# Two expert layers with a dense gate map: another layout of the map in PSUM, another plan of the choose stage, and later gathered sums

## The chip, the cores and the metric

The kernel runs on one core of a Trainium2 chip. A core has five engines with a queue each: TensorE (PE; its weight loads are shown apart as PEld), VectorE (DVE), ScalarE (ACT), GpSimd (POOL) and SyncE (SP, which here only issues DMAs). They share the on-chip memory SBUF; matrix products land in PSUM, eight banks of 2 KiB per partition, from where VectorE and ScalarE read them. The metric is the device time of one execution in microseconds; a time is the median of several runs.

## The reference

Two blocks work on 512 tokens of width 1024, in float32: the first with gated linear attention and a sliding window, the second with two other attentions. Each ends in a PEER layer, and the change lies there. A layer has 8 heads, and each head picks 16 of 128 x 128 = 16384 experts, so that every token has 128 experts with a gate each:

```python
def peer_layer(xn, w_pq, sub_keys, expert_u, expert_v):
    ...
    scores = jnp.einsum('thpd,hpkd->thpk', qp, sub_keys).astype(jnp.float32)
    s_top, i_top = lax.top_k(scores, PEER_TOPK)
    cand = (s_top[:, :, 0, :, None] + s_top[:, :, 1, None, :]).reshape(t, PEER_HEADS, PEER_TOPK * PEER_TOPK)
    cand_idx = (i_top[:, :, 0, :, None] * PEER_NKEYS + i_top[:, :, 1, None, :]).reshape(...)
    best, pos = lax.top_k(cand, PEER_TOPK)
    idx = jnp.take_along_axis(cand_idx, pos, axis=-1)
    gate = jax.nn.softmax(best, axis=-1).astype(xn.dtype)
    ...
        u = expert_u[ib]
        h = jax.nn.gelu(jnp.einsum('lkd,ld->lk', u, xb), approximate=False)
        return jnp.einsum('lk,lkd->ld', gb * h, expert_v[ib])
```

## The kernel before

**Two ways through the experts.** For the first 384 tokens (TD) a layer goes through all 16384 experts densely: 128 chunks of 128 experts. For each chunk it multiplies the chunk of u with the tokens, applies gelu, multiplies with a map of gates that is zero where a token has not picked an expert, and multiplies the result with the chunk of v. The last 128 tokens are done by gathering: four sets of 32 tokens, whose 128 experts per token are fetched by indirect DMAs, 32 fetches of u rows and 32 of v rows per set (NSET = 4, tile `gr`).

**Split operands.** Dense products are made of float32 operands in two parts, a high part rounded to the format fp32r, and a low part, the rest. `mm3` (lines 285 to 287) issues three matmuls: high by high, low by high, high by low. One chunk of u is a *unit* of 8 x 3 = 24 matmuls of 128x384. Its weights are split when they have come in: ScalarE writes the high part (`whi`, line 222), and VectorE or GpSimd the low part (`wlo`, line 231). `unit` keeps one split unit ahead.

**choose**, once per layer, has three sorts of work that run beside each other:
- `best` finds the top 16 of the scores on VectorE, and `select` (one call per 128 tokens, `pick` around it) the 16 of 256 candidates, with their two keys i1 and i2 and the gates, all on VectorE. Its `turn` transposes keys and gates on TensorE (float32, three transposes), and ScalarE and VectorE write them as i1T, i2T and the high and low parts of the gate, ghi and glo.
- `maps` builds the gate map in halves of 16 tokens, 24 halves per layer. `one_hots` makes four tables per half on VectorE (lines 1258, 1259, 1261, 1262): `o1`, `ah`, `al`, `o2`, the last of which is shown as `o` at line 1262. `gate_map` then issues 32 matmuls of 128x128 in fp16 (lines 1275 and 1276) into four banks `pg`, four tokens in each, and after each bank ScalarE copies it into `stage` (line 1278). Two halves make a `stage`, which goes to DRAM.
- `uahead` does 56 of the 128 u chunks ahead of the main loop, 52 of them in choose, so that TensorE has work while VectorE selects. The low part is made by VectorE except where the call says GpSimd.

**What sets the order.** Every engine runs its queue in order, and choose writes the queues by a plan: `tv` and `tp` are the expected times of VectorE and TensorE. After each piece of `select` or `one_hots` the generator yields its cost, `tv` grows by it, and `fill(tv - behind)` issues units (4.2 each) until TensorE's time has come up; `flush` then issues the TensorE work that VectorE has prepared (`turn`, and `dense` at 1.9). `force` issues waiting work at once where a buffer must come free.

**main_loop** has 131 steps, one for each v unit (two chunks' halves) and for the late u chunks, 72 of 128. A step in order: `weigh` (line 1637, the low part `wl` of the weighted activations of the step before, on VectorE, after ScalarE's high part `wh` of line 1690), `low_u` (line 1589, the low part of the next late unit, on VectorE), `high_v`, issues of gathers, one gathered step, `low_v` (line 1610), the unit's matmuls, more gathered steps, the weighting by the map (line 1687), then the products with v, and `flush_later`. A gathered step is a reduction over the fetched u row (line 1319) or an accumulation of the fetched v row (line 1331, tile `acc`) on VectorE. After the last accumulation of a set `fin` sums the partitions by quads on TensorE (line 1338, 8 small matmuls) and VectorE adds the result to xT (`upd_t`: line 443 in the first layer, 470 in the second). `fin` is handed to `soon`, and runs at the next `flush_later`: at the end of the step, or at once when the next set's first step (`ustep` with j = 0) comes up.

Of the kernel before, what the change touches and what calls it, by code (L numbers as in the profile page):

```python
# [8 lines left out]
F32 = mybir.dt.float32  # L9
# [168 lines left out]
class Kern:  # L178
    def __init__(self, ctx, tc, ins, cat, outs, upto, dbg):
        self.ctx, self.tc, self.nc = ctx, tc, tc.nc  # L180
        self.ins, self.cat, self.outs, self.upto, self.dbg = ins, cat, outs, upto, dbg
        self.alt, self.alt2 = 0, 0

        self.ahead = [c for c in range(P) if c // 4 % 2 == 0 and c < 112]
        self.late = [c for c in range(P) if c not in self.ahead]
        self.ua_last = 4
        self.ua_end, self.behind = 6, 0.5
# [962 lines left out]
    def select(self, i, sv, si, sp, sp2, out, later, force):  # L1150
# [47 lines left out]
        V.tensor_tensor(t1[:, 0:8], ge, dl[:, :, :, None].to_broadcast(B4), op=ALU.mult)  # L1198
        V.tensor_tensor(t1[:, 8:16], ge, self.offD[:, None, :, :].to_broadcast(B4), op=ALU.mult)
        yield 3.4  # L1200
        for w in (8, 4, 2):
            V.tensor_add(t1[:, :, 0:w, :], t1[:, :, 0:w, :], t1[:, :, w:2 * w, :])
        yield 2.4
        i1 = sp.tile([P, 8, 16], F32, tag="i1", name="i1")
        i2 = sp.tile([P, 8, 16], F32, tag="i2", name="i2")
# [5 lines left out]
                        op=ALU.is_equal)  # L1211
        yield 2.3
        V.tensor_tensor(ge, ge, ix[:, :, 1, :, None].to_broadcast(B4), op=ALU.mult)
# [3 lines left out]
        yield 4.0  # L1217
# [3 lines left out]
        V.tensor_tensor(gate, gate, sm[:, :, None].to_broadcast([P, 8, 16]), op=ALU.mult)  # L1221
        yield 0.8
# [12 lines left out]
        def turn():  # L1235
            pt = self.pb()
            for n, src in enumerate((i1, i2, gate)):
                self.transpose(pt[:, n * P:(n + 1) * P], src.rearrange("p a b -> p (a b)"))
            s = slice(i * P, (i + 1) * P)
            i1T, i2T, ghi, glo = out  # L1240
# [8 lines left out]
    def one_hots(self, t0, sel, sp, sp2, made):  # L1249


        V = self.nc.vector
        B4 = [P, 8, P, 2]
        io = self.iotaM[:, None, :, :].to_broadcast(B4)
        i1T, i2T, ghi, glo = [t[:, t0:t0 + 16].rearrange("p (q f) -> p q f", f=2)[:, :, None, :] for t in sel]
# [4 lines left out]
        yield 2.4  # L1260
        V.tensor_tensor(al, o1, glo.to_broadcast(B4), op=ALU.mult)  # L1261
        V.tensor_tensor(o2, io, i2T.to_broadcast(B4), op=ALU.is_equal)  # L1262
        yield 2.3
        made += [ah, al, o2]

    def gate_map(self, oh, stage, half):

        S, PE = self.nc.scalar, self.nc.tensor
        ah, al, o2 = oh
        for q in range(4):  # L1270
            pg = self.pb()
            for f in range(4):
                o = pg.rearrange("p (i f) -> p i f", f=4)[:, :, f]
                n, m = 2 * q + f // 2, f % 2
                PE.matmul(o, ah[:, n, :, m], o2[:, n, :, m], start=True, stop=False)  # L1275
                PE.matmul(o, al[:, n, :, m], o2[:, n, :, m], start=False, stop=True)
            tt = half * 16 + q * 4
            S.activation(stage[:, :, tt:tt + 4], pg.rearrange("p (i f) -> p i f", f=4), AF.Copy, scale=2.0 ** -15)

    def gather_steps(self, h, un, vn, gw, gb, upd_t):  # L1280
# [5 lines left out]
        for n in range(NSET):  # L1286
# [37 lines left out]
            def vstep(j, n=n, t0=t0, st=st):  # L1324
# [9 lines left out]
                if j == 31:  # L1334
# [7 lines left out]
                    self.soon(fin)  # L1342
# [31 lines left out]
    def choose(self, h, hd, nq, scores, keys_src, pu, hscr, gscr, steps, prep, gelp, mk2):  # L1374
# [6 lines left out]
        self.bank, self.soon, self.flush_later = self.pb, lambda f: f(), lambda: None  # L1381
# [4 lines left out]
        sel = [cst.tile([P, T], F16, name=n) for n in ("i1T", "i2T", "ghi", "glo")]  # L1386
# [9 lines left out]
        def uahead(eng=V):  # L1396
            nonlocal ahead, tp, tv
            ph = self.pa()
# [79 lines left out]
        del qall, keys  # L1478
        for t, n in ((self.offM, "off"), (self.offD, "offd"), (self.iotaJ, "iota16")):
            V.tensor_copy(t, self.c(n)[:, :, None].to_broadcast([P, 16, 16]))  # L1480
# [52 lines left out]
    def main_loop(self, h, pu, pv, upd, steps, start_next, finish, gscr, hscr, uahead, pools):  # L1533

# [90 lines left out]
        def flush_later():  # L1625
            while later:
                later.pop(0)()

        self.bank, self.soon, self.flush_later = lambda: turn(ubank), later.append, flush_later
# [27 lines left out]
        for s in range(NC + 3):  # L1657
# [4 lines left out]
            weigh()  # L1662
# [5 lines left out]
            gathered(min(qs, nd + 1))  # L1668
            low_v(s - 2)
# [28 lines left out]
            flush_later()  # L1698
# [553 lines left out]
```

## Time and profile before

| what | value |
|---|---|
| median of 3 runs | 3509.58 us (3507.26 to 3523.71) |
| profiled execution, its own time | 3514.7 us |
| span of that execution | 3512.9 us |
| TensorE busy | 3373.0 us, 96% |
| its weight loads (beside it) | 2950.5 us, 84% |
| VectorE busy | 2602.4 us, 74% |
| ScalarE busy | 1357.5 us, 39% |
| GpSimd busy | 926.6 us, 26% |
| choose of the first layer, from its last top-k on | 676 to 1009 us |
| choose of the second layer, likewise | 2280 to 2609 us |

The profile is one execution, taken by the hardware profiler. A row of the waits names the engine and line that waited, what it waited for, and the time in total, the number of waits and the longest. A row of a stretch gives the busy time of TensorE, the weight loads, VectorE, ScalarE and GpSimd with the number of instructions in brackets, then the clock granted to TensorE as a share of the full one, the share of the DMA engines' time, and GB/s. A row in time begins with the start and the duration in us; matmuls are pipelined, so that the distance of two starts tells their rate and the duration does not. `pb<-o,ah` reads: writes tile pb, reads o and ah; L is a line of the kernel.

### The profile page before, as it was taken

The page shows a single profiled execution, that of the slowest core. Times are in us where ns is not written, and L with a number is a line of the kernel's source. Part 1 is how long each engine was busy: PE and PEld are TensorE (multiplying, and loading weights), DVE is VectorE, ACT ScalarE, POOL GpSimd, SP SyncE. Part 2 cuts the span into 40 slices and gives each one's busy share as a digit, 9 for nine tenths or more (in the row PEclk, how much of TensorE's full clock was granted, in tenths as well). Part 3 has the DMA queues.
Part 4 walks back from the last instruction along what each step waited for, and adds up shares of the span by engine and source line. Part 5 has one row for each costly group of instructions (what it writes and reads, how often), then busy time and mean ns, then how long its engine had stood idle before and what let it go on. Part 6 is the DMA issues. An engine that isn't in the chain of part 4 may idle for free. (4 is left out here: it accounts for less than half of the span.)

```text
span 3512.9 us, 48336 instructions
## 1 busy us (share of the span) xinstructions
PE 3373.0 (96%) x17772; PEld 2950.5 (84%) x17772; DVE 2602.4 (74%) x5342; ACT 1357.5 (39%) x2497; POOL 926.6 (26%) x792
## 2 busy tenths in 40 slices
PE   9999999899989999999999999989989999999998
PEld 7768888799978888888888768879978888888887
DVE  4466665778878887888864685788878878788873
ACT  4445223234443333333334444324443333333332
POOL 1422004200013433443422401400004434344431
PEclk9999999999999999999999999999999999999999
DMA  4211673255689999899972201235689999899971
GB/s 135 78 37 47 237 249 102 78 184 183 213 290 345 328 347 332 318 351 330 355 259 77 78 19 39 79 130 186 210 259 351 354 334 335 327 343 335 350 296 66
DMA packets 321790, 787.49 MB, mean 224 GB/s; under 512 B 27392, under 2 KB 156800, under 8 KB 321424
## 3 DMA queue, kind: packets, MB, share of 16 engines
q1 hardware_dynamic: 247568, 515.36, 40.8%
q0 software_dynamic: 73984, 269.05, 22.1%
q8 instruction: 139, 2.28, 0.3%
q14 instruction: 99, 0.81, 0.1%
HBM read 709.59 MB, written 74.45 MB: 223 GB/s over the span
## 5 line engine op out<-in xcount | busy, mean ns | idle before, releaser
L1311 POOL DMA_INDIRECT gr<-in_pn_dram,gset x256 | 316.6, 1237 | 1149.4 <-DVE hd L1319 926.5
L287 PE MATMUL pa<-hh,wlo 128*128 128x384 f32 (+2 forms) x1536 | 545.9, 355 | 43.3 <-DVE wlo L231 42.3
L285 PE MATMUL pa<-hh,whi 128*128 128x384 f32 (+2 forms) x1536 | 550.6, 358 | 5.8 <-ACT whi L222 4.0
L286 PE MATMUL pa<-hl,whi 128*128 128x384 f32 (+2 forms) x1536 | 543.9, 354 | 5.9 <-POOL hl L544 4.8
L1311 POOL DMA_INDIRECT gr<-in_pm_dram,gset x256 | 328.2, 1282 | 439.7 <-DVE acc L1331 293.2
L285 PE MATMUL pa<-vh,wh 128*128 128x512 f32 x1024 | 401.9, 392 | 0.0
L286 PE MATMUL pa<-vl,wh 128*128 128x512 f32 x1024 | 400.9, 392 | 0.4 <-DVE vl L1610 0.4
L287 PE MATMUL pa<-vh,wl 128*128 128x512 f32 x1024 | 400.7, 391 | 0.0
L287 PE MATMUL pb<-hh,wlo 128*128 128x384 f32 x1152 | 389.3, 338 | 5.2 <-DVE wlo L1589 3.9
L231 DVE TENSOR_TENSOR wlo<-wraw,whi 128x1024 fp32r<-128x1024 f32 x189 | 234.7, 1243 | 213.9 <-ACT whi L222 213.3
L285 PE MATMUL pb<-hh,whi 128*128 128x384 f32 x1152 | 392.0, 340 | 0.5 <-ACT whi L1583 0.5
L286 PE MATMUL pb<-hl,whi 128*128 128x384 f32 x1152 | 388.5, 337 | 0.0
L287 PEld LDWEIGHTS pa<-hh,wlo 128*128 128x128 f32 x1536 | 293.8, 191 | 72.5 <-DVE wlo L231 49.5
L1610 DVE TENSOR_TENSOR vl<-vraw,vh 128x512 fp32r<-128x512 f32 x512 | 333.3, 692 | 5.0 <-ACT vh L1602 5.0
L1331 DVE SCALAR_TENSOR_TENSOR acc<-gr,hd,acc 128x1024 f32<-128x1024 f32 x248 | 317.8, 1281 | 24.9 <-DMA gr<-in_pm_dram,gset 23.3
L1319 DVE CUSTOM_DVE_ANT_0 gr<-gr,ht 128x1024 f32<-128x1024 f32 x256 | 309.3, 1220 | 19.8 <-DMA gr<-in_pn_dram,gset 19.8
L285 PEld LDWEIGHTS pa<-hh,whi 128*128 128x128 f32 x1536 | 294.4, 192 | 30.5 <-ACT whi L222 5.5
L286 PEld LDWEIGHTS pa<-hl,whi 128*128 128x128 f32 x1536 | 293.7, 191 | 29.3 <-POOL hl L544 6.3
L1602 ACT CAST vh<-vraw 128x512 fp32r<-128x512 f32 x512 | 291.7, 618 | 0.8 <-PE pb L287 0.7
L222 ACT CAST whi<-wraw 128x1024 fp32r<-128x1024 f32 x243 | 253.7, 1044 | 79.3 <-PE pa L286 39.1
L1690 ACT CAST wh<-gel 128x384 fp32r<-128x384 f32 x144 | 73.9, 513 | 426.6 <-DVE gel L1687 426.0
L287 PEld LDWEIGHTS pa<-vh,wl 128*128 128x128 f32 x1024 | 193.1, 189 | 40.6
(443 smaller groups left out, 6723.9 us busy)
## 6 DMA issues: line engine op xcount, KB each, us to landing
vraw<-in_pv_dram SPq DMA_DIRECT2D x256, 512.0 KB
uraw<-in_pu_dram SPq DMA_DIRECT2D x138, 512.0 KB
wraw<-in_pu_dram SPq DMA_DIRECT2D x118, 512.0 KB
wraw<-in_wT_dram SPq DMA_DIRECT2D x97, 512.0 KB
gscrp<-stage SPq DMA_DIRECT2D x24, 2048.0 KB
gt<-gscrp SPq DMA_DIRECT2D x64, 768.0 KB
ada<-in_wadaT_dram SPq DMA_DIRECT2D x48, 512.0 KB
hscrp<-gel SPq DMA_DIRECT2D x112, 192.0 KB
```

Of the source, the lines that this page charges most:

```text
L222: self.nc.scalar.copy(hi, raw)
L231: lo_eng.tensor_sub(lo, raw, hi.bitcast(F32))
L285: nc.tensor.matmul(out, l[0], r[0], start=start, stop=False, **kw)
L286: nc.tensor.matmul(out, l[0], r[1], start=False, stop=False, **kw)
L287: nc.tensor.matmul(out, l[1], r[0], start=False, stop=stop, **kw)
L1311: G.indirect_dma_start(out=u, out_offset=None, in_=tab, in_offset=bass.IndirectOffsetOnAxis(ap=self.gset[n][:, 1, j:j + 1].bitcast(I32), a ...
L1319: V.tensor_tensor_reduce(u, u, st["ht"], 1.0, 0.0, ALU.mult, ALU.add, st["hd"][:, j:j + 1])
L1331: V.scalar_tensor_tensor(st["acc"], v, w, st["acc"], op0=ALU.mult, op1=ALU.add)
L1602: S.copy(hi, vraw[u][:, c * 512:(c + 1) * 512])
L1610: V.tensor_sub(lo, raw[:, c * 512:(c + 1) * 512], vs[u][c].bitcast(F32))
L1690: S.copy(wh, gel)
```

## The change

1. In `gate_map` each token's 128 columns go to PSUM next to each other; before, the four tokens of a bank were interleaved word by word. ScalarE's copy reads the bank with the other stride, so that `stage` is the same.
2. `select` writes keys and the two parts of the gate in fp16 itself, and `turn` turns the four by fp16 matmuls against an identity, with one ScalarE copy into one tile `sel`. Before: three float32 transposes, three ScalarE copies, one VectorE operation.
3. The plan: `select` and `one_hots` yield more often, the cost is taken at 1.0 in place of 1.05, `behind` is 1.5 in place of 0.5.
4. `uahead` gives the low part to GpSimd when `tv` is over `tp` by more than 2.8.
5. `fin` is issued three steps later, at the end of a step.
6. `weigh` stands behind the step's first gathered step, in place of ahead of `low_u`.

```diff
@@ select
         V.tensor_tensor(t1[:, 0:8], ge, dl[:, :, :, None].to_broadcast(B4), op=ALU.mult)
+        yield 2.25
         V.tensor_tensor(t1[:, 8:16], ge, self.offD[:, None, :, :].to_broadcast(B4), op=ALU.mult)
-        yield 3.4
+        yield 1.2
...
-        i1 = sp.tile([P, 8, 16], F32, tag="i1", name="i1")
-        i2 = sp.tile([P, 8, 16], F32, tag="i2", name="i2")
+        i1, i2, gh, gl = [sp.tile([P, 8, 16], F16, tag=n, name=n) for n in ("i1", "i2", "gh", "gl")]
...
+        if i * P < TD:
+            V.tensor_scalar(gh, gate, 32768.0, None, op0=ALU.mult)
+            V.scalar_tensor_tensor(gl, gate, 32768.0, gh, op0=ALU.mult, op1=ALU.subtract)
...
         def turn():
             pt = self.pb()
-            for n, src in enumerate((i1, i2, gate)):
-                self.transpose(pt[:, n * P:(n + 1) * P], src.rearrange("p a b -> p (a b)"))
...
-            S.copy(i1T[:, s], pt[:, 0:P])
-            S.copy(i2T[:, s], pt[:, P:2 * P])
-            S.activation(ghi[:, s], pt[:, 2 * P:3 * P], AF.Copy, scale=32768.0)
-            V.scalar_tensor_tensor(glo[:, s], pt[:, 2 * P:3 * P], 32768.0, ghi[:, s], op0=ALU.mult, op1=ALU.subtract)
+            for n, src in enumerate((i1, i2, gh, gl)):
+                PE.matmul(pt[:, n * P:(n + 1) * P], src.rearrange("p a b -> p (a b)"), self.ident16, start=True, stop=True)
+            S.copy(out[:, :, i * P:(i + 1) * P], pt.rearrange("p (a b) -> p a b", b=P))
@@ one_hots
         V.tensor_tensor(o1, io, i1T.to_broadcast(B4), op=ALU.is_equal)
+        yield 1.25
         V.tensor_tensor(ah, o1, ghi.to_broadcast(B4), op=ALU.mult)
-        yield 2.4
+        yield 1.15
         V.tensor_tensor(al, o1, glo.to_broadcast(B4), op=ALU.mult)
+        yield 1.15
         V.tensor_tensor(o2, io, i2T.to_broadcast(B4), op=ALU.is_equal)
-        yield 2.3
+        yield 1.15
@@ gate_map
             for f in range(4):
-                o = pg.rearrange("p (i f) -> p i f", f=4)[:, :, f]
+                o = pg[:, f * P:(f + 1) * P]
...
-            S.activation(stage[:, :, tt:tt + 4], pg.rearrange("p (i f) -> p i f", f=4), AF.Copy, scale=2.0 ** -15)
+            S.activation(stage[:, :, tt:tt + 4], pg.rearrange("p (f i) -> p i f", f=4), AF.Copy, scale=2.0 ** -15)
@@ gather_steps
-                    self.soon(fin)
+                    self.soon(fin, 3)
@@ choose
-        def uahead(eng=V):
+        def uahead(eng=None):
             nonlocal ahead, tp, tv
+            eng = eng or (G if tv > tp + 2.8 else V)
...
             for cost in f(i):
-                tv += cost * 1.05
+                tv += cost
@@ main_loop
-        def flush_later():
-            while later:
-                later.pop(0)()
+        def soon(f, n=0):
+            later.append([n, f])
+
+        def flush_later(step=0):
+            for e in list(later):
+                if e[0] <= 0:
+                    later.remove(e)
+                    e[1]()
+                e[0] -= step
...
-            weigh()
             low_u(s + 1)
...
             gathered(min(qs, nd + 1))
+            weigh()
...
-            flush_later()
+            flush_later(1)
```

How the queues change is shown at three places. A row is a line of the kernel, an operation, what it writes and reads, and its shape. First VectorE in the first layer's choose, at the thirteenth and fourteenth half of the gate map (the tables o, ah, al of `one_hots` and low parts wlo), before:

```order
L231 TENSOR_TENSOR wlo<-wraw,whi 128x1024
L1261 TENSOR_TENSOR al<-o_8213,glo 128x2048
L1262 TENSOR_TENSOR o_8216<-iotaM,i2T 128x2048
L1258 TENSOR_TENSOR o_8296<-iotaM,i1T 128x2048
L1259 TENSOR_TENSOR ah<-o_8296,ghi 128x2048
L1261 TENSOR_TENSOR al<-o_8296,glo 128x2048
L1262 TENSOR_TENSOR o_8299<-iotaM,i2T 128x2048
L1258 TENSOR_TENSOR o_8345<-iotaM,i1T 128x2048
L1259 TENSOR_TENSOR ah<-o_8345,ghi 128x2048
L1261 TENSOR_TENSOR al<-o_8345,glo 128x2048
L1262 TENSOR_TENSOR o_8348<-iotaM,i2T 128x2048
```

and after:

```order
L1257 TENSOR_TENSOR o_8065<-iotaM,sel 128x2048
L1259 TENSOR_TENSOR ah<-o_8065,sel 128x2048
L1261 TENSOR_TENSOR al<-o_8065,sel 128x2048
L1263 TENSOR_TENSOR o_8068<-iotaM,sel 128x2048
L231 TENSOR_TENSOR wlo<-wraw,whi 128x1024
L1257 TENSOR_TENSOR o_8148<-iotaM,sel 128x2048
L1259 TENSOR_TENSOR ah<-o_8148,sel 128x2048
L1261 TENSOR_TENSOR al<-o_8148,sel 128x2048
L1263 TENSOR_TENSOR o_8151<-iotaM,sel 128x2048
L231 TENSOR_TENSOR wlo<-wraw,whi 128x1024
```

Before, the low parts end here, and the second half follows the first with no unit between; after, a low part stands behind each half, so that TensorE has a unit between two halves. Over the whole choose TensorE's last run of halves with no unit between has 14 halves before and 6 after in the first layer, 16 and 9 in the second.

Second GpSimd, from the last operation ahead of the first layer's choose to the first set of gathers (wlo are low parts, gr the fetched rows), before:

```order
L1298 TENSOR_TENSOR hr<-hh,hl 128x128
L231 TENSOR_TENSOR wlo<-wraw,whi 128x1024 x10
L1311 DMA gr<-in_pn_dram,gset_4703 128x1024 x32
L1311 DMA gr<-in_pm_dram,gset_4703 128x1024 x32
L1311 DMA gr<-in_pn_dram,gset_4704 128x1024 x32
L1311 DMA gr<-in_pm_dram,gset_4704 128x1024 x32
```

and after:

```order
L1299 TENSOR_TENSOR hr<-hh,hl 128x128
L231 TENSOR_TENSOR wlo<-wraw,whi 128x1024 x18
L1312 DMA gr<-in_pn_dram,gset_4703 128x1024 x5
L231 TENSOR_TENSOR wlo<-wraw,whi 128x1024 x3
L1312 DMA gr<-in_pn_dram,gset_4703 128x1024 x27
L1312 DMA gr<-in_pm_dram,gset_4703 128x1024 x32
```

Eleven more low parts stand here, eight ahead of the first fetch and three behind the fifth. In the second layer there are as many; on VectorE as many fewer, 171 in place of 193 over the kernel.

Third VectorE in the main loop, where the second set of gathered tokens in the first layer ends (line 443 adds the quad sums to xT), before:

```order
L1687 TENSOR_TENSOR gel<-gel,gt 128x384
L1637 TENSOR_TENSOR wl<-gel,wh 128x384
L1589 TENSOR_TENSOR wlo<-uraw,whi 128x1024
L1331 SCALAR_TENSOR_TENSOR acc<-gr,hd,acc 128x1024
L1610 TENSOR_TENSOR vl<-vraw,vh 128x512 x2
L1331 SCALAR_TENSOR_TENSOR acc<-gr,hd,acc 128x1024
L443 TENSOR_TENSOR xT<-pb,xT 128x8x32
L1319 ISA gr,hd<-gr,ht 128x1024
L1319 ISA hd 128x1
L1687 TENSOR_TENSOR gel<-gel,gt 128x384
L1637 TENSOR_TENSOR wl<-gel,wh 128x384
```

and after, from the same step on:

```order
L1699 TENSOR_TENSOR gel<-gel,gt 128x384
L1594 TENSOR_TENSOR wlo<-uraw,whi 128x1024
L1332 SCALAR_TENSOR_TENSOR acc<-gr,hd,acc 128x1024
L1649 TENSOR_TENSOR wl<-gel,wh 128x384
L1615 TENSOR_TENSOR vl<-vraw,vh 128x512 x2
L1332 SCALAR_TENSOR_TENSOR acc<-gr,hd,acc 128x1024
...
L1615 TENSOR_TENSOR vl<-vraw,vh 128x512 x2
L1699 TENSOR_TENSOR hb<-hb,gt 128x384
L443 TENSOR_TENSOR xT<-pb,xT 128x8x32
L1320 ISA gr,hd<-gr,ht 128x1024
```

The addition of line 443 has moved from right behind the last accumulation to 22 rows later. At the head of the step wl (line 1637, after: 1649) stood ahead of the low part wlo (1589, after: 1594), and now stands behind it and behind one accumulation.

## Rows read from the trace of the kernel before

**Rows 1.** waits of TensorE, whole span: total us, times, longest us
```profile
PE pa L287 <- DVE wlo L231: 42.3, 17, 15.6
PE pb L1275 <- DVE o L1262: 28.3, 26, 1.5
PE pb L1338 <- DVE acc L1331: 17.8, 5, 6.1
PE pb L287 <- DVE wlo L1589: 3.9, 2, 2.0
```

**Rows 2.** stretches of choose: us, then busy us by engine, clock, DMA share, GB/s
```profile
676.00:1009.00 333.00, 302.03 (x1987) 293.98 (x1986) 276.21 (x660) 140.52 (x219) 7.51 (x6) 0.97 0.59 187
2280.00:2609.00 329.00, 292.32 (x1925) 282.97 (x1924) 282.87 (x728) 137.04 (x215) 12.65 (x7) 0.98 0.58 184
680.00:720.00 40.00, 26.16 (x140) 25.84 (x139) 26.92 (x146) 7.14 (x10) 0.00 (x0) 0.83 0.28 93
2290.00:2330.00 40.00, 24.40 (x131) 23.95 (x130) 28.48 (x163) 6.32 (x10) 0.00 (x0) 0.83 0.28 92
760.00:780.00 20.00, 16.50 (x79) 15.87 (x79) 16.53 (x45) 7.49 (x11) 6.96 (x5) 0.83 0.80 266
```

**Rows 3.** waits of TensorE in 676:1009, then in 2280:2609; columns as in 1
```profile
PE pa L287 <- DVE wlo L231: 18.1, 5, 13.8
PE pb L1275 <- DVE o L1262: 11.8, 11, 1.1
...
PE pa L287 <- DVE wlo L231: 19.1, 5, 15.6
PE pb L1275 <- DVE o L1262: 16.5, 15, 1.5
```

**Rows 4.** TensorE in time at 858.6 us, and line 1275's loads (ns min/median/max)
```profile
858.57 0.34 PE L286 MATMUL pa<-hl,whi 128*128 128x384 f32 x1
...
858.92 0.28 PE L1275 MATMUL pb<-o,ah 128*128 128x128 f16 x1
859.00 0.31 PE L1276 MATMUL pb<-o,al 128*128 128x128 f16 x1
859.11 0.31 PE L1275 MATMUL pb<-o,ah 128*128 128x128 f16 x1
...
L1275 PEld LDWEIGHTS <-ah x768: 96/135/135, 835.9 to 2610.1; 128*128 128x128 f16 x192
```

**Rows 5.** line 1278 on ScalarE: ns min/median/max
```profile
L1278 ACT ACTIVATE stage<-pb x192: 597/598/602, 837.0 to 2610.6; 128x512 f32<-128x512 f32 x192
```

**Rows 6.** VectorE in time in the first layer's tail of choose
```profile
967.73 1.22 DVE L1258 TENSOR_TENSOR o<-iotaM,i1T 128x2048 f16<-128x2048 f16 x1
...
972.47 1.22 DVE L1258 TENSOR_TENSOR o<-iotaM,i1T 128x2048 f16<-128x2048 f16 x1
```

**Rows 7.** line 231 by engine: ns min/median/max, first and last start
```profile
L231 DVE TENSOR_TENSOR wlo<-wraw,whi x189: 1205/1226/1660, 12.2 to 2639.4; 128x1024 fp32r<-128x1024 f32 x189
L231 POOL TENSOR_TENSOR wlo<-wraw,whi x48: 2349/2406/2852, 60.8 to 2285.3; 128x1024 fp32r<-128x1024 f32 x48
```

**Rows 8.** VectorE, then GpSimd, in time near 1880 us; line 1610 on the page
```profile
1881.79 4.68 DVE L1610 TENSOR_TENSOR vl<-vraw,vh 128x512 fp32r<-128x512 f32 x2 [1.64 <-ACT vh L1602]
...
1880.72 5.21 POOL L231 TENSOR_TENSOR wlo<-wraw,whi 128x1024 fp32r<-128x1024 f32 x2 [79.20 <-PE pb L287]
...
L1610 DVE TENSOR_TENSOR vl<-vraw,vh 128x512 fp32r<-128x512 f32 x512 | 333.3, 692 | 5.0 <-ACT vh L1602 5.0
```

**Rows 9.** stretches of the main loops; columns as in 2
```profile
1200.00:1250.00 50.00, 47.58 (x230) 41.55 (x230) 40.10 (x61) 18.32 (x35) 19.34 (x16) 0.97 0.92 339
1400.00:1450.00 50.00, 43.86 (x208) 38.60 (x207) 37.26 (x56) 17.03 (x32) 18.30 (x15) 0.93 0.81 296
...
3400.00:3450.00 50.00, 48.42 (x245) 44.05 (x244) 24.63 (x35) 16.07 (x29) 0.00 (x0) 0.97 0.39 136
```

**Rows 10.** waits of VectorE, whole span: total us, times, longest us
```profile
DVE wl L1637 <- ACT wh L1690: 199.1, 252, 3.5
```

More of the change, by code (lines that the diff above doesn't have):

```diff
@@ L186, in __init__ @@
         self.ua_last = 4
-        self.ua_end, self.behind = 6, 0.5
+        self.ua_end, self.behind = 6, 1.5
     def dump(self, name, t):
@@ L1198, in select @@
         V.tensor_tensor(t1[:, 0:8], ge, dl[:, :, :, None].to_broadcast(B4), op=ALU.mult)
+        yield 2.25
         V.tensor_tensor(t1[:, 8:16], ge, self.offD[:, None, :, :].to_broadcast(B4), op=ALU.mult)
-        yield 3.4
+        yield 1.2
         for w in (8, 4, 2):
             V.tensor_add(t1[:, :, 0:w, :], t1[:, :, 0:w, :], t1[:, :, w:2 * w, :])
-        yield 2.4
-        i1 = sp.tile([P, 8, 16], F32, tag="i1", name="i1")
-        i2 = sp.tile([P, 8, 16], F32, tag="i2", name="i2")
+            yield 0.8
+        i1, i2, gh, gl = [sp.tile([P, 8, 16], F16, tag=n, name=n) for n in ("i1", "i2", "gh", "gl")]
         jr = sp.tile([P, 8, 16], F16, tag="jr", name="jr")
@@ L1211, in select @@
                         op=ALU.is_equal)
+        yield 2.0
+        V.tensor_tensor(ge, ge, ix[:, :, 1, :, None].to_broadcast(B4), op=ALU.mult)
         yield 2.3
-        V.tensor_tensor(ge, ge, ix[:, :, 1, :, None].to_broadcast(B4), op=ALU.mult)
         for w in (8, 4, 2):
@@ L1216, in select @@
         V.tensor_add(i2, ge[:, :, 0, :], ge[:, :, 1, :])
-        yield 4.0
+        yield 1.9
         force(exp)
@@ L1236, in turn @@
             pt = self.pb()
-            for n, src in enumerate((i1, i2, gate)):
-                self.transpose(pt[:, n * P:(n + 1) * P], src.rearrange("p a b -> p (a b)"))
-            s = slice(i * P, (i + 1) * P)
-            i1T, i2T, ghi, glo = out
-            S.copy(i1T[:, s], pt[:, 0:P])
-            S.copy(i2T[:, s], pt[:, P:2 * P])
-            S.activation(ghi[:, s], pt[:, 2 * P:3 * P], AF.Copy, scale=32768.0)
-            V.scalar_tensor_tensor(glo[:, s], pt[:, 2 * P:3 * P], 32768.0, ghi[:, s], op0=ALU.mult, op1=ALU.subtract)
+            for n, src in enumerate((i1, i2, gh, gl)):
+                PE.matmul(pt[:, n * P:(n + 1) * P], src.rearrange("p a b -> p (a b)"), self.ident16, start=True, stop=True)
+            S.copy(out[:, :, i * P:(i + 1) * P], pt.rearrange("p (a b) -> p a b", b=P))
         if i * P < TD:
@@ L1254, in one_hots @@
         io = self.iotaM[:, None, :, :].to_broadcast(B4)
-        i1T, i2T, ghi, glo = [t[:, t0:t0 + 16].rearrange("p (q f) -> p q f", f=2)[:, :, None, :] for t in sel]
+        i1T, i2T, ghi, glo = [sel[:, n, t0:t0 + 16].rearrange("p (q f) -> p q f", f=2)[:, :, None, :] for n in range(4)]
         o1 = sp.tile(B4, F16, tag="o1", name="o1")
@@ L1380, in choose @@
         cst = mk2("selc", 1)
-        self.bank, self.soon, self.flush_later = self.pb, lambda f: f(), lambda: None
+        self.bank, self.soon, self.flush_later = self.pb, lambda f, n=0: f(), lambda: None
         self.offM = cst.tile([P, 16, 16], F16, name="offM")
@@ L1385, in choose @@
         self.iotaM = cst.tile([P, P, 2], F16, name="iotaM")
-        sel = [cst.tile([P, T], F16, name=n) for n in ("i1T", "i2T", "ghi", "glo")]
+        sel = cst.tile([P, 4, T], F16, name="sel")
+        self.ident16 = cst.tile([P, P], F16, name="ident16")
         sv = [cst.tile([P, 8, 2, 16], F32, name=f"sv{i}") for i in range(4)]
@@ L1478, in choose @@
         del qall, keys
+        V.tensor_copy(self.ident16, self.c("ident"))
         for t, n in ((self.offM, "off"), (self.offD, "offd"), (self.iotaJ, "iota16")):
@@ L1623, in main_loop @@
         later = []
-        def flush_later():
-            while later:
-                later.pop(0)()
-        self.bank, self.soon, self.flush_later = lambda: turn(ubank), later.append, flush_later
+        def soon(f, n=0):
[6 more added lines that the diff above has]
+                e[0] -= step
+        self.bank, self.soon, self.flush_later = lambda: turn(ubank), soon, flush_later
         weights = []
@@ L1697, in main_loop @@
                 del vs[s - 4]
-            flush_later()
+            flush_later(1)
+        assert not later
         ubank.clear()
```

1 line of the change is left out of this document (removed).

## The prediction

> **What bounds the kernel now.** I read the page first, then the waits of TensorE, then short stretches around its longest waits, and only then single instructions. TensorE is busy nearly all the time, so the span is its work plus its idle time plus what a lowered clock costs. The waits [rows 1] name where it idles: 42.3 us for low parts on line 231, 28.3 us for the last one-hot table (line 1262), 17.8 us for the gathered accumulator (line 1331), 3.9 us for the late low parts (line 1589). The first two lie in choose. There TensorE is busy 302 of 333 us in the first layer and 292 of 329 in the second, with VectorE at 276 and 283 [rows 2], so VectorE is the engine that sets it waiting: once for 13.8 us and once for 15.6 us, and then 11 and 15 times for about 1.1 us each [rows 3]. [...]
>
> **Part 1, maps apart in PSUM.** Before, each 128-column matmul of the gate map writes every fourth word. Its starts are 80 ns apart for the first pair of a half and 110 ns from then on (859.00 to 859.11; I use 109, the mean of the whole half), and the weight load grows from 96 to 135 ns [rows 4]. A load that starts at once in the first pair and is held in the later ones speaks for the array being held by its output rather than by its weights. After, the output is contiguous. What one then takes the trace does not show; I bound it by 109 ns (nothing gained, weights are the limit) and 56 ns (the 128 columns alone: a 128x384 matmul starts every (858.92 - 858.57) / 2 = 0.175 us [rows 4], a third of which is 58), and take 80, the unheld first pair. There are 24 halves x 32 = 768 per layer, 1536 in all: 1536 x (109 - 80) = 44.5 us, all of it on TensorE.
> [...]
> The copy out of PSUM (line 1278) now reads with a step of 512 bytes. It takes 598 ns [rows 5], four in a half, on ScalarE that is busy 141 of 333 us [rows 2]: hidden unless it doubles. The price of a strided read is not in the trace; zero is taken, and the far end is a rival.
>
> **Part 2, keys and gates turned in fp16.** Six selects lose three transposes, two small ScalarE copies and one VectorE operation that read PSUM, and gain four 128-column matmuls and two small VectorE operations. TensorE gains 6 instructions of some 0.1 us. Nothing within the error; the one thing of worth is that VectorE no longer waits for a transpose in the middle of its queue.
>
> **Parts 3 and 4, plan and low parts.** 22 low parts (11 per layer) leave VectorE (1.23 us each) for GpSimd (2.41 us each) [rows 7]: VectorE gets 13.5 us per layer. With the finer steps the units are spread differently: the last run of halves with no unit between them on TensorE shrinks from 14 to 6 in the first layer and from 16 to 9 in the second. In such a run VectorE sets the pace, 972.47 - 967.73 = 4.74 us per half (four tables) [rows 6]. Before, TensorE needs 32 x 109 ns = 3.5 and waits 1.1 to 1.2, as seen. After it needs 32 x 80 ns = 2.56 and waits 2.2, so part of the gain of part 1 is given back here: with the first two halves of each run ready ahead, 4 and 7 waits, 8.7 and 15.3 us, against 11.8 and 16.5 before.
> The long waits (13.8 and 15.6 us) come from low parts queued on VectorE behind the last top-k. With 4 of them on GpSimd, which makes one in 2.4 us while a unit takes 24 x 0.175 = 4.2 us, TensorE has work for most of this. It does not vanish, since the first low part left on VectorE still stands behind the top-k: I take a third, 4.7 us, and half the clock loss, 3.4 us. Bounds: 0 and all of it.
> What speaks against it: near 1880 us two subtractions on VectorE took 4.68 us instead of 2 x 0.69 beside two low parts on GpSimd [rows 8], so 1.65 us lost per GpSimd part. [...] For 11 parts that is 18 us of VectorE per layer at most, and more than the 13.5 it is given; the top-k operations beside two of GpSimd's low parts were not slower, TensorE does not wait for VectorE everywhere, and I count a third, 6 us. Three of the eleven stand behind five gathers in GpSimd's queue, which wait for the selected sets; a unit is made ahead, so I count that at nothing (up to 4 us per layer).
> First layer: idle and clock before 18.1 + 11.8 + 6.8 + 3.4 = 40.1, after 4.7 + 3.4 + 8.7 + 6 = 22.8, gain 17.3. Second: before 19.1 + 16.5 + 6.8 = 42.4, after 4.7 + 3.4 + 15.3 + 6 = 29.4, gain 13.0. Together 30.3 us.
>
> **Part 5, gathered sums three steps later.** Four times per layer TensorE's quad sums (line 1338) stand in its queue ahead of a step's products, and TensorE waits for the accumulator: 17.8 us in five waits [rows 1]. Each lowers the clock after it: five stretches of 50 us with 0.97, 0.93, 0.93, 0.90 and 0.97 granted, of which the first two and the last stand in [rows 9]; 0.30 x 50 = 15 us. Three steps later the accumulator has long been done, and products run meanwhile. Gain 32.8 us, from bounds of 0 (the wait turns up elsewhere) and 32.8. What is late next: the update of xT on VectorE (line 443, or 470) then waits for the sums at a place of its own in VectorE's queue, with the low part of the next unit and the v halves behind it. VectorE is busy 37 of 50 us [rows 9], so a wait of one step there is covered.
>
> **Part 6, weigh after the first gathered step.** Line 1637 waits for ScalarE 252 times, 199.1 us in all [rows 10], 0.8 us each, at the head of a step, with the low part of the next unit behind it. Moved behind that part and one gathered operation of 1.2 us, this wait is gone. It reaches TensorE only in the 3.9 us of line 1589 [rows 1]: gain 3.9 us, bounds 0 and 8 with its clock. Its own reader is four steps away.
>
> **Sum.** 44.5 + 30.3 + 32.8 + 3.9 = 111.5 us. From the profiled execution, 3514.7 us, this gives 3403.2; that execution lies 5.1 us above the median of the runs, 3509.58, and so the forecast is 3398 us, a gain of 3.2%. About 0.5% (17.5 us) is what a measurement of this kernel can tell from no change.
>
> **Rivals.**
> *Weights are the limit, the dense half stays at 109 ns.* Part 1 is then nothing, and the tail's waits are 1.1 instead of 2.2 us: 111.5 - 44.5 + 11 x 1.1 = 79 us, 3431 us. For it: 135 ns of load in each steady pair. Against: 96 ns when not held.
> *Columns alone are the limit, 56 ns.* 1536 x 53 = 81.4 instead of 44.5, less 11 x 0.77 = 8.5 us more waiting in the tails: 140 us, 3370 us. For it: loads run beside matmuls. Against: the first pair's 80 ns.
> *GpSimd's low parts lock VectorE out each time.* 36 us for both layers where I count 12: 3422 us, and with the clock behind such waits some 3435. For it: the row at 1880 us. Against: VectorE's work beside most of these parts is top-k.
> *The strided read binds, and the kernel is slower.* Per half and unit ScalarE has 4 copies of r plus (141 - 96 x 0.6) / 56 = 1.5 us for the unit's split and gelu [rows 2, 5]; TensorE has 2.56 + 4.2 = 6.8 us. Above r = 1.3 us ScalarE sets the pace of 48 halves, at 192 x (r - 1.3). To eat the whole gain r must be 1.9 us, 3.2 times the 598 ns [rows 5]; at 2.1 us 192 x 0.8 = 154, and the time is 3552 us. Nothing in the trace shows such a copy; it decides from 1.9 us on.
> *It does less than it says.* The sums merely move TensorE's wait into VectorE's queue, and low parts do not relieve choose, with only some of part 1 left: 3495 us.
>
> **How the numbers follow.** Forecast (3380 to 3420): 0.55. Columns alone, 3370: 0.16. Weights, 3431: 0.12. Lock, 3435: 0.10. Little of it, 3495: 0.04. Slower, 3552: 0.03. Range: down past the case at 56 ns with the choose waits gone too, 3358; up past lock and weights, 3440. Faster than 3492 holds 0.93, within 0.5% 0.04, slower 0.03.
>
> **What would show it.** Right: dense starts near 80 ns and loads near 96; no wait of TensorE on the accumulator, and no stretch of the main loop under 0.97 granted; the longest wait on line 231 under 6 us; 10 to 12 waits on the last one-hot table, each longer than before. Wrong: starts still at 109; line 1278 over 0.6 us by much; VectorE subtractions of 3 us beside GpSimd's; waits of TensorE for low parts made on GpSimd; a new wait of VectorE for the quad sums followed by one of TensorE on line 1589's successor. The forecast fails most easily in part 1, where one row carries 44.5 us, and in the third that I leave of the long waits.

## The result and the profile after

| | before | after |
|---|---|---|
| median | 3508.42 us (4 runs) | 3396.45 us (3392.24 to 3398.12, 4 runs) |
| profiled execution | 3514.7 us | 3398.12 us |
| span of it | 3512.9 us | 3396.4 us |

The ratio is 0.9671 (95% interval 0.9641 to 0.9700), a gain of 3.3%; forecast were 3398 us and 3.2%. The time is right to two microseconds, and that closeness is luck: two terms of the sum were mis-sized in opposite directions, and a third stood under the wrong part, as the rows and runs below show.

The waits of TensorE after (total us, times, longest us), to be read beside [rows 1]:

```profile
PE pb L1276 <- DVE o L1263: 26.7, 15, 2.7
PE pa L287 <- DVE wlo L231: 16.5, 13, 6.3
PE pa L287 <- POOL wlo L231: 9.3, 8, 2.8
PE pb L347 <- POOL ssq L339: 7.4, 3, 2.6
PE pb L1242 <- DVE gl L1225: 6.5, 2, 3.5
```

No row names the accumulator any more (17.8 us before) nor the late low parts (3.9 us). The waits for VectorE's low parts fell from 42.3 to 16.5 us, the longest from 15.6 to 6.3. The wait for the last one-hot table is nearly as long in total as before, 26.7 against 28.3 us, in fewer and longer pieces. Two rows are new or grown: low parts made by GpSimd (0.9 us before), and the low part of the gates (`gl`) for the fp16 turn.

The gate map in time, one half outside the last run and its loads (start us, duration us; then ns min/median/max), to be read beside [rows 4]:

```profile
830.71 0.23 PE L1276 MATMUL pb<-o,ah 128*128 128x128 f16 x1
830.78 0.22 PE L1277 MATMUL pb<-o,al 128*128 128x128 f16 x1
830.84 0.22 PE L1276 MATMUL pb<-o,ah 128*128 128x128 f16 x1
830.90 0.22 PE L1277 MATMUL pb<-o,al 128*128 128x128 f16 x1
...
L1276 PEld LDWEIGHTS <-ah x768: 96/97/146, 806.4 to 2512.3; 128*128 128x128 f16 x192
```

Starts are 60 to 70 ns apart in these first rows, and 58 in the mean of a half, where they were 109; the loads are 97 ns in the median in place of 135. ScalarE's copy with the new step is as long as before, 598 ns [rows 5]:

```profile
L1279 ACT ACTIVATE stage<-pb x192: 588/598/622, 807.1 to 2512.8; 128x512 f32<-128x512 f32 x192
```

The two main loops from their first to their last product with v: two stretches of before, then two of after (columns as in [rows 2]):

```profile
1043.80:1899.30 855.50, 840.92 (x4114) 744.98 (x4113) 671.71 (x985) 305.77 (x553) 318.53 (x253) 0.99 0.85 313
2644.60:3493.20 848.60, 837.86 (x4115) 743.58 (x4114) 670.40 (x998) 303.97 (x551) 316.34 (x251) 0.99 0.85 313
```

```profile
1000.10:1832.20 832.10, 831.41 (x4115) 738.62 (x4115) 667.09 (x987) 307.66 (x555) 339.88 (x253) 1.00 0.88 323
2544.10:3376.70 832.60, 831.40 (x4115) 738.57 (x4114) 667.75 (x1002) 306.71 (x554) 330.51 (x251) 1.00 0.87 320
```

After, TensorE is busy in all of both loops (831.4 of 832.1 and of 832.6 us) at the full clock (1.00, before 0.99). They gave 23.4 + 16.0 = 39.4 us. The rest of the span's gain of 116.5 us is 77 us: the stretch to the first product gave 43.7 and that between the loops 33.4. Each holds one of the two choose stages.

### The profile page after: what moved, and what is told of

Read it like the earlier page. It is cut to its first block, busy times and chain, and to the rows that moved or that the text cites. A ratio compares the mean times of both kernels' runs of the same rounds, so it can differ in the third digit from the quotient of the medians.

```text
span 3396.4 us, 48502 instructions
## 1 busy us (share of the span) xinstructions
PE 3297.4 (97%) x17778; PEld 2877.0 (85%) x17778; DVE 2588.8 (76%) x5328; ACT 1344.0 (40%) x2485; POOL 1021.4 (30%) x814
## 5 line engine op out<-in xcount | busy, mean ns | idle before, releaser
L287 PE MATMUL pa<-hh,wlo 128*128 128x384 f32 (+2 forms) x1536 | 548.4, 357 | 26.4 <-DVE wlo L231 16.5
L1312 POOL DMA_INDIRECT gr<-in_pn_dram,gset x256 | 295.0, 1152 | 706.0 <-DVE hd L1320 657.0
L1312 POOL DMA_INDIRECT gr<-in_pm_dram,gset x256 | 380.8, 1487 | 383.5 <-DVE acc L1332 242.8
L231 POOL TENSOR_TENSOR wlo<-wraw,whi 128x1024 fp32r<-128x1024 f32 x70 | 179.7, 2568 | 576.6 <-ACT whi L222 565.4
L231 DVE TENSOR_TENSOR wlo<-wraw,whi 128x1024 fp32r<-128x1024 f32 x167 | 207.7, 1244 | 162.8 <-ACT whi L222 162.1
L1687 ACT ACTIVATE gel<-pb 128x384 f32<-128x384 f32 x144 | 70.9, 492 | 501.6 <-PE pb L287 498.8
```

Of the source, the lines that this page charges most:

```text
L231: lo_eng.tensor_sub(lo, raw, hi.bitcast(F32))
L287: nc.tensor.matmul(out, l[1], r[0], start=False, stop=stop, **kw)
L1312: G.indirect_dma_start(out=u, out_offset=None, in_=tab, in_offset=bass.IndirectOffsetOnAxis(ap=self.gset[n][:, 1, j:j + 1].bitcast(I32), a ...
L1687: S.activation(gel, ph[:, :TD], AF.Gelu)
```

## The experiments

Medians are of four runs, of five in the last experiment; ratios are to the kernel before, on the same chip. Chips differ: the kernel before stood between 3508 and 3517 us on them. So a difference between two of these runs is known to some 12 us, by the intervals of their ratios.

### Part 1 alone

```diff
-                o = pg.rearrange("p (i f) -> p i f", f=4)[:, :, f]
+                o = pg[:, f * P:(f + 1) * P]
...
-            S.activation(stage[:, :, tt:tt + 4], pg.rearrange("p (i f) -> p i f", f=4), AF.Copy, scale=2.0 ** -15)
+            S.activation(stage[:, :, tt:tt + 4], pg.rearrange("p (f i) -> p i f", f=4), AF.Copy, scale=2.0 ** -15)
```

> The kernel before with part 1 alone: the four tokens of a bank next to each other in PSUM, the plan and all else as before. Theory (the plan decides how much part 1 is worth): matmuls of the gate map start every 58 ns in place of 109, so a half is 1.6 us shorter, but only where a unit or a wait of TensorE's own follows; the last 14 and 16 halves are paced by VectorE at 4.74 us each and gain nothing. 10 + 8 halves outside these runs x 1.6 = 29 us, to about 3479 us, and TensorE's waits on the last one-hot table grow from 1.1 to 2.7 us, with a lowered clock in the runs. Rival (part 1 is worth the same anywhere): 1536 x 51 ns = 78 us, 3430 us.

Measured: 3488.32 us, ratio 0.9927 (0.9902 to 0.9952): 23 to 26 us less, not 78. TensorE's largest wait is now this (it was 28.3 us in 26 waits), and below it stands the last run of the first layer's halves, from its first half on, once of this kernel and once of the kernel before (stretches as in [rows 2]):

```profile
PE pb L1275 <- DVE o L1262: 57.0, 29, 3.2
...
931.00:991.00 60.00, 36.35 (x447) 33.86 (x445) 56.67 (x49) 30.56 (x56) 0.00 (x0) 0.80 0.80 243
```

```profile
947.00:1007.00 60.00, 48.24 (x426) 44.91 (x424) 56.20 (x49) 31.48 (x54) 0.00 (x0) 1.00 0.78 237
```

In the run the first matmuls of the halves still start 4.74 us apart, VectorE's pace [rows 6]. What the matmuls save there, TensorE waits, and its granted clock falls from 1.00 to 0.80 in addition. So part 1 pays only in halves outside these runs.

### All but part 1

The same two lines turned back in the changed kernel:

```diff
-                o = pg[:, f * P:(f + 1) * P]
+                o = pg.rearrange("p (i f) -> p i f", f=4)[:, :, f]
...
-            S.activation(stage[:, :, tt:tt + 4], pg.rearrange("p (f i) -> p i f", f=4), AF.Copy, scale=2.0 ** -15)
+            S.activation(stage[:, :, tt:tt + 4], pg.rearrange("p (i f) -> p i f", f=4), AF.Copy, scale=2.0 ** -15)
```

> The changed kernel with part 1 taken back: map interleaved in PSUM as before, all else changed. Theory (the plan decides): starts every 109 ns again; 18 + 15 halves outside the last runs x 1.6 us = 54 us more, in the last runs nothing, and some of the lowered clock there comes back (up to 10 us): 3440 to 3450 us. Rival (worth the same anywhere): 78 us more, 3474 us.

Measured: 3450.38 us, ratio 0.9832 (0.9815 to 0.9848). The 54 us more are about 33 halves x 1.6 us, the upper end of the theory's range; the rival's 78 us are excluded. The granted clock rose, from 0.984 to 0.991 in the mean of the profiled executions, and TensorE's waits for the last one-hot table fell from 26.7 to 10.7 us: in the last runs the longer matmuls mostly fill time in which TensorE waited. Part 1 is worth 54 us here and 23 to 26 us on the kernel before: a second sign that its worth depends on the plan.

### Parts 2, 3 and 4 alone

The kernel before with the fp16 turns, the finer plan and the rule for low parts:

```diff
-        self.ua_end, self.behind = 6, 0.5
+        self.ua_end, self.behind = 6, 1.5
...
-        def uahead(eng=V):
+        def uahead(eng=None):
...
+            eng = eng or (G if tv > tp + 2.8 else V)
...
-                tv += cost * 1.05
+                tv += cost
```

> The kernel before with parts 2, 3 and 4 alone (fp16 turns, the finer plan, low parts by the free engine): map interleaved in PSUM, sums at once and weigh first as before. Part 1 alone gave 23 us, and parts 1 to 4 together (the run with parts 5 and 6 taken back) 80 us. Theory (each needs the other: shorter matmuls pay only where a unit follows, and the plan puts one there): the plan alone gives about 27 us, as the forecast worked out for it (30), so 3480 to 3486 us, and 30 us of the 80 belong to the pair. Rival (the two are independent): 80 - 23 = 57 us, 3453 us.

Measured: 3493.36 us, ratio 0.9930 (0.9905 to 0.9955), about 24 us less, which agrees with the theory's 27 and is far from the rival's 57. Together with the run below that takes parts 5 and 6 both back this makes a square: part 1 alone 0.7%, the plan alone 0.7%, both 2.15%. Some 25 us by the ratios, or 33 of the 80 by the medians, belong to neither alone (about 17 us either way, by the intervals). The plan puts a unit behind more of the halves, and shorter matmuls then bring the unit forward; without it they end in a wait. Parts 2 and 3 were not run by themselves.

### Parts 5 and 6: one back, the other back, both back, one alone

Sums at once again:

```diff
-                    self.soon(fin, 3)
+                    self.soon(fin)
```

> The changed kernel with part 5 taken back: quad sums issued at the next flush, ahead of a step's products. Theory: TensorE waits again for the accumulator about 18 us in five waits and loses 15 us to the clock: 33 us more, 3429 us. Rival (moving the step's other VectorE work, part 6, had already taken these waits away): 3396 us, no wait on line 1332. Second rival (the delay costs VectorE something of its own, which is given back here): under 20 us.

Measured: 3402.36 us, ratio 0.9692 (0.9675 to 0.9710): 6 us more than the changed kernel, not 33, and no more than such a difference leaves open. The first main loop is as long as with the delay, 832.1 us, with no wait on the accumulator in it. In the second one wait is left, and that loop is 838.1 us long in place of 832.6:

```profile
PE pb L1339 <- DVE acc L1332: 2.1, 1, 2.1
```

So the first rival holds but for this one wait.

Weigh first again:

```diff
             low_u(s + 1)
...
             gathered(min(qs, nd + 1))
-            weigh()
...
+            weigh()
             low_u(s + 1)
```

> The changed kernel with part 6 taken back: weigh at the head of a step again, ahead of low_u. Theory: VectorE waits for ScalarE some 0.8 us per step again, about 200 us in all, and TensorE sees two waits of about 2 us on the late low parts: 4 us more, 3400 us. Rival (VectorE has been the reserve that the later sums need, so that the waits spread): 10 to 20 us more.

Measured: 3408.94 us, ratio 0.9710 (0.9694 to 0.9726): 12 us more: within the rival's range, though the interval alone does not exclude the theory's 4. The first main loop of the profiled execution is 841.9 us long in place of 832.1. VectorE's 200.8 us of waits for ScalarE are back, and TensorE's waits on the late low parts are 5.5 us in seven, no longer two.

Both back:

> The changed kernel with parts 5 and 6 both taken back. Alone, part 5 taken back cost 6 us and part 6 taken back 12 us. Theory (either part takes away the waits on the accumulator, since either gives VectorE its time: the 200 us of waits at the head of the steps, or three steps): both back bring the waits of about 18 us in five and the 15 us of lowered clock, 35 to 45 us more than 3396, 3431 to 3441 us. Rival (they are independent): 6 + 12 = 18 us more, 3414 us.

Measured: 3430.59 us, ratio 0.9785 (0.9751 to 0.9820): 34 us more than the changed kernel, where 6 + 12 would be 18. The waits on the accumulator are back (line 1339 is line 1338 of before):

```profile
PE pb L1339 <- DVE acc L1332: 15.6, 5, 6.3
```

Part 6 alone, on the kernel before:

```diff
-            weigh()
             low_u(s + 1)
...
             gathered(min(qs, nd + 1))
+            weigh()
```

> The kernel before with part 6 alone: weigh behind the first gathered step, sums issued as before. Theory (as above, part 6 by itself is enough): the waits on the accumulator go, 17.8 us and 15 us of clock, and 3.9 us on line 1589: 30 to 40 us less than before, 3470 to 3480 us, main loops of about 832 and 838 us from first to last product. Rival (the forecast's sum: part 6 is worth its 4 us): 3505 us.

Measured: 3476.36 us, ratio 0.9900 (0.9877 to 0.9924): 34 us less from a part that the forecast had at 4. Its two main loops, its quad sums, and its wait of VectorE on `wl`, which was 199.1 us in 252 waits [rows 10]:

```profile
1044.00:1878.60 834.60, 833.08 (x4115) 739.73 (x4115) 666.54 (x986) 306.30 (x553) 341.86 (x253) 1.00 0.87 321
2623.70:3456.20 832.50, 831.27 (x4115) 738.60 (x4115) 668.91 (x1002) 306.82 (x555) 334.06 (x251) 1.00 0.87 320
...
its engine sat idle before it (us, times) until:
  ACT gel L1675: 1.1, 1
  DVE acc L1331: 0.8, 1
...
DVE wl L1637 <- ACT wh L1690: 3.0, 5, 0.7
```

Both loops are within 3 us of the changed kernel's, with the sums still issued at once. TensorE waits 0.8 us for the accumulator. So VectorE was late with it because at the head of each step it stood 0.8 us waiting for ScalarE, and then spent 0.56 us on `wl` itself, in front of work that was ready. The run moves both together, and the wait is the larger. Take it away and the accumulator is in time; take it away or give the sums three steps, either does it.

### Part 4: how many low parts GpSimd makes

Four runs alter the rule or its inputs in the changed kernel; the plan's two numbers, altered in the second, also set when units are issued. No low part by the rule:

```diff
-            eng = eng or (G if tv > tp + 2.8 else V)
+            eng = eng or V
```

> The changed kernel with part 4 taken back: low parts of choose on VectorE wherever the call does not name GpSimd, so 22 fewer on GpSimd. The plan then has last runs of 10 and 14 halves in place of 6 and 9. Theory (GpSimd relieves VectorE): VectorE has 11 x 1.23 = 13.5 us more per layer, the long waits for the first low part come back with their clock, and longer runs are paced by VectorE: 25 to 40 us more, 3421 to 3436 us. Rival (GpSimd's low parts lock VectorE out for as long as they save): within 10 us of 3396 us.

The two numbers of the plan as before, which leaves the rule little to give away:

```diff
-        self.ua_end, self.behind = 6, 1.5
+        self.ua_end, self.behind = 6, 0.5
...
-                tv += cost
+                tv += cost * 1.05
```

> The changed kernel with the two numbers of the plan as before (costs times 1.05, behind 0.5), the finer yields and the rule for GpSimd kept. The rule then sends only 6 more low parts to GpSimd than before the change, in place of 22, and the last runs have 12 and 15 halves. Theory (what counts is how many low parts leave VectorE, and the numbers do it through the rule): close to the run with all low parts on VectorE, less some 4 us per layer: 3417 to 3430 us. Rival (the rule alone does it, the numbers are fine tuning): under 3405 us.

A lower threshold, and a much lower one (1.0 in the same place):

```diff
-            eng = eng or (G if tv > tp + 2.8 else V)
+            eng = eng or (G if tv > tp + 2.4 else V)
```

> The changed kernel with the rule's threshold at 2.4 in place of 2.8: 23 more low parts on GpSimd (93 in place of 70), and the last runs of halves with no unit between go from 6 to 1 and from 9 to 5. Theory (a low part on GpSimd locks VectorE's two-input operations out for about as long as it saves): TensorE's waits move from the last one-hot table to GpSimd's low parts, 3390 to 3405 us. Rival (the runs at the end are what is left to gain): half of the 26.7 us of waits there and 10 us of their clock go, 3375 us.

> The changed kernel with the threshold at 1.0: 62 more low parts on GpSimd than in the changed kernel (132), no run of halves without a unit at the end, but 13 and 10 units left over behind the last half. Theory (lock): 62 x (2.2 - 1.2) = 60 us more on VectorE, of which TensorE sees a half: 3415 to 3445 us. Rival (VectorE relieved is all that counts): 62 x 1.2 = 74 us less on VectorE, and TensorE never waits: 3370 us.

Measured:

| low parts on GpSimd more than before | 0 | 6 | 22 (the change) | 45 | 84 |
|---|---|---|---|---|---|
| us | 3414.29 | 3406.78 | 3396.45 | 3421.38 | 3460.27 |
| ratio | 0.9724 | 0.9711 | 0.9671 | 0.9734 | 0.9847 |
| 95% interval | 0.9701 to 0.9747 | 0.9686 to 0.9735 | 0.9641 to 0.9700 | 0.9713 to 0.9755 | 0.9826 to 0.9867 |
| VectorE busy on its low parts (line 231), us | 234.7 | 227.5 | 207.7 | 180.9 | 132.3 |
| VectorE busy in select and one_hots (lines 1162 to 1263), us | 369.0 | 369.3 | 396.5 | 433.0 | 512.5 |

The first two are 18 and 10 us above the change, below the 25 to 40 and 21 to 34 that were expected; with some 12 us of doubt the rivals (within 10 us, and under 9) are not excluded. More than 22 makes it slower, beyond both expectations at 2.4: 3421 us where 3390 to 3405 stood. At 1.0 it is 15 us above the end of the range.

The last two rows of the table, added up from the traces, show what the lock (the slowing of VectorE and GpSimd beside each other) costs VectorE. The 22 low parts take 27.0 us off VectorE, and its own work in choose grows by 27.5 us: it is not relieved at all. At 45 and 84 it gives up more than it is given (64 for 54 us, and 143 for 102). So the 22 do not pay by VectorE's time but by their place: with none, TensorE waits up to 15.7 us for one low part, as before the change (15.6), and with 22 up to 6.3 us, and the last runs are shorter (6 and 9 halves against 10 and 14). How much of the loss at 45 and 84 is the lock and how much is later turns and low parts, these runs do not separate.

The waits of the run with no low part by the rule:

```profile
PE pb L1276 <- DVE o L1263: 44.2, 22, 2.7
PE pa L287 <- DVE wlo L231: 34.4, 11, 15.7
```

Where the lock sits is seen in the changed kernel itself: GpSimd beside the first select, then VectorE there, then the halving additions of select over all calls (before: 291/426/694 ns):

```profile
691.88 2.40 POOL L231 TENSOR_TENSOR wlo<-wraw,whi 128x1024 fp32r<-128x1024 f32 x1 [1.81 <-ACT whi L222]
700.18 3.38 POOL L231 TENSOR_TENSOR wlo<-wraw,whi 128x1024 fp32r<-128x1024 f32 x1 [5.91 <-ACT whi L222]
...
756.43 4.21 POOL L231 TENSOR_TENSOR wlo<-wraw,whi 128x1024 fp32r<-128x1024 f32 x1 [15.45 <-ACT whi L222]
...
758.45 3.53 DVE L1216 TENSOR_TENSOR ge<-ge 128x1024 f16<-128x1024 f16 x3
...
L1216 DVE TENSOR_TENSOR ge<-ge x24: 291/426/2743, 729.4 to 2422.4; 128x1024 f16<-128x1024 f16 x8, 128x512 f16<-128x512 f16 x8, 128x256 f16<-128x256 f16 x8
```

Beside the top-k (up to 698 us) a low part takes 2.40 us. Beside select the two engines hold each other: GpSimd's part takes up to 4.21 us in place of 2.41, and an addition of VectorE up to 2.74 us, where the longest before was 0.69. Seven of the eleven parts that the rule moves in a layer are longer than 2.5 us. At 1.0 TensorE waits for GpSimd's parts themselves, and for the one-hot tables more than before though no long run is left:

```profile
PE pb L1276 <- DVE o L1263: 50.8, 22, 3.6
PE pa L287 <- POOL wlo L231: 36.6, 17, 10.1
```

### A version that beats both

From this, only the first five low parts of each choose by the rule:

```diff
-            eng = eng or (G if tv > tp + 2.8 else V)
+            if eng is None:
+                eng = G if tv > tp + 2.8 and len(given) < 5 else V
+                given += [1] if eng is G else []
```

> The changed kernel, but the rule gives GpSimd only the first five low parts in each choose, which run beside the last top-k, and leaves the other six to VectorE. Runs with 6, 22, 45 and 84 more low parts on GpSimd than before stood at 3407, 3396, 3421 and 3460 us; this one has 10. Theory (only the low parts beside select and the one-hot tables lock VectorE out, those beside the top-k are free): the six cost VectorE 6 x 1.23 = 7.4 us per layer and give back some 20 us of locks over both layers, so 3390 to 3398 us, in spite of last runs of 8 and 12 halves. Rival (the low parts beside select pay as well, and the shorter last runs with them): 3402 to 3408 us, between the runs with 6 and 22.

Measured: 3383.76 us (3382.78 to 3386.86, 5 runs), ratio 0.9630 (0.9615 to 0.9644), 12.7 us under the changed kernel (14 by the ratios) and 6 us past the range's best end. Its waits:

```profile
PE pb L1276 <- DVE o L1263: 34.9, 17, 2.7
PE pa L287 <- DVE wlo L231: 9.5, 9, 4.1
...
PE pa L287 <- POOL wlo L231: 5.4, 4, 2.3
```

The last runs are longer again (8 and 12 halves) and the wait there grows by 8 us; the waits for low parts and for the turn shrink by 17. The mechanism is the one expected: VectorE's busy time in select and one_hots is 372.7 us, 23.8 less than in the changed kernel, where some 20 us of locks were to come back. The expectation was not exact on one point: in each layer three of the five parts stand beside the top-k, and the last two already beside select (3.34 and 2.83 us long in the first layer, 5.10 and 2.83 in the second).

## Why the prediction came out right, and where its steps did not

- **What bounds it: right.** TensorE's work, its idle time and the clock behind it account for the change; the span became shorter by 116.5 us.
- **Part 1: mechanism right, size wrong.** The output held the array: with a token's columns next to each other the starts are 58 ns apart in place of 109. The step that failed is the choice of 80 ns from the first pair of a half: it is 58 ns, the end that was given as "columns alone" (by its own row 58 and not the 56 that it put there), so 1536 x 51 = 78 us of TensorE's work at the full clock in place of 44.5. The 80 ns came from one pair at the head of a half, the only sample, and were no rate. What the array saved in the last runs of halves was not gained, as the coupling in parts 3 and 4 said: VectorE paces them at 4.74 us. About a tenth of the starts, all in these runs, are even 107 ns apart again, at the lower clock, 0.50 from 953 to 958 us:

```profile
955.68 0.31 PE L1276 MATMUL pb<-o,ah 128*128 128x128 f16 x1
955.79 0.31 PE L1277 MATMUL pb<-o,al 128*128 128x128 f16 x1
955.90 0.31 PE L1276 MATMUL pb<-o,ah 128*128 128x128 f16 x1
```

- **Strided copy on ScalarE: right.** 598 ns as before; that rival is out.
- **Parts 3 and 4: direction right, size wrong on its own terms.** The long waits went as forecast (2.8 and 6.3 us remain where 4.7 each stood). But the forecast kept only these two of the waits on line 231 and let the shorter ones go without a reason: 16.5 + 9.3 = 25.8 us are left where it had 9.4. The waits in the last runs are longer than the 24 us forecast, 26.7, since halves are shorter, and bring lowered clock with them, 0.87 and 0.81 in these two stretches, where before it was 1.00:

```profile
940.00:980.00 40.00, 30.38 (x280) 29.17 (x279) 28.17 (x25) 18.24 (x31) 0.00 (x0) 0.87 0.87 269
2470.00:2515.00 45.00, 29.28 (x323) 27.46 (x322) 40.42 (x36) 22.16 (x39) 0.00 (x0) 0.81 0.76 232
```

  That clock costs little there, since VectorE paces the halves anyway, at 4.74 us. The idle time and clock of the two stages gave almost nothing in total, in place of 30.3 us, and the matmuls nearly all. So the step that failed here is that the idle time and its clock would shrink by 30.3 us: the waits were spread, and the lowered clock moved into the last runs. The two errors cancel in the sum, and that is luck: 44.5 + 30.3 = 74.8 us forecast, 77 measured. But the experiments show that this is not an attribution: either half alone gives 23 to 24 us, and the rest needs both.

  No run shows the 6.8 us a layer and the 3.4 us that the forecast takes as lost to the clock: they were the author's estimates, 0.17 x 40 and 0.17 x 20 us, from the 0.83 of [rows 2]. The trace of the kernel before shows 0.50 granted from 690 to 703.4, 2301 to 2314.4 and 771.8 to 778.4 us, with TensorE busy for 4.8, 3.2 and 5.3 us of them; an estimate from these is half of each, 2.4, 1.6 and 2.6 us. After the change the stretches of 690 to 730 and 2236 to 2276 us were granted 0.91 and 0.87.
- **The lock: right as a mechanism.** Beside select a low part on GpSimd took up to 4.21 us in place of 2.41. Its row at 1880 us [rows 8] was the one to extend: of the numbers tried 22 parts pay and 45 do not, and 10 better placed ones pay more. That TensorE sees one third of the worst, 12 us, was a guess. On VectorE the lock took 27.5 us over both layers, where the forecast put the worst at 36; what of it reached TensorE was not measured by itself.
- **Not foreseen: the turn.** TensorE waits 6.5 us in two waits for `gl` (line 1225), which part 2 was said not to cost. Part 2 does not cost them: in the runs with 0, 6 and 10 low parts more on GpSimd, which all have part 2, this wait does not occur at all, and in that with 45 the turn's waits are 17.9 us. They come with the further low parts beside select.
- **Parts 5 and 6: sum right, attribution wrong.** 32.8 + 3.9 = 36.7 us forecast, 39.4 measured. The step that failed is that part 6 "reaches TensorE only in the 3.9 us of line 1589". VectorE's wait at the head of a step, 0.8 us, held up the accumulations behind it too, and these were what the quad sums waited for. Part 6 alone gives 34 us; part 5, given part 6, 6 us (without part 6 it is 3430.59 - 3408.94 = 22 us; alone on the kernel before it was not run).
- **What is late next: right.** VectorE now waits for the quad sums 21.8 us at line 443 and 22.9 us at line 470, in four waits each (10.2 and 10.4 before), and no wait of TensorE follows.
- **The signs it named.** Loads at 97 ns, no wait on the accumulator and main loops at the full clock came as said. Starts at 58 ns in place of 80, a longest wait of 6.3 us on line 231 where under 6 stood, and 15 waits on the last one-hot table where 10 to 12 stood did not. TensorE's waits for GpSimd's low parts, 9.3 us in eight, stood among the signs of being wrong.

## What to carry to other kernels

When two edits touch the same wait, price them as a pair: here two edits took away the same wait, and each of two others was worth a third of what both gave. The wait of 0.8 us at the head of VectorE's queue in each step was charged to everything that stood behind it (moving it gave 34 us by itself), so follow the queue to the last instruction that another engine waits for before calling it hidden. Work moved to a second engine was cheap here only beside instructions that it did not slow and that did not slow it (a low part on GpSimd took 2.40 us beside the top-k, up to 4.21 beside select): choose the place first, then the number, and add up the first engine's busy time over all of its work, since here it was given 27 us and lost as much.

## What the runs showed of the hardware that was not expected

A stream of a load and a 128-column fp16 matmul in turn ran at 58 ns a pair, though one load lasted 97 ns in the median: loads overlapped each other and the matmuls. With the output at every fourth word of PSUM the same stream took 109 ns, and its loads 135. And the lock between VectorE and GpSimd worked in both directions: beside select GpSimd's subtraction took up to 4.21 us in place of 2.41, and VectorE's additions up to 2.74 us, where the longest before was 0.69.
